# Layer 0's keys and values by seven sub-products, in the order that layer 1 has

## The chip, the core and the metric

The kernel runs on one core of one Trainium2 chip. Five engines work side by side and wait for one another by semaphores: TensorE (PE, matmuls; PEld is its weight load), VectorE (DVE), ScalarE (ACT), GpSimd (POOL, here mostly an issuer of DMAs) and SyncE (SP, the other issuer of DMAs). The metric is the device time of one launch in microseconds; lower is better.

## The reference

Two layers of a decoder on 512 tokens of width 1024, all in float32. The part that the change touches is the attention branch of a layer and what lies around it:

```python
mod = (c_act @ w_ada + b_ada)[:, None, :]
sh1, sc1, g1, sh2, sc2, g2 = jnp.split(mod, 6, axis=-1)
h = rmsnorm(x, norm1_w) * (1 + sc1) + sh1
u = h @ w_in
u_pool, u_conv, b_conv, c_conv, q, k, v, gate_logits = jnp.split(u, offsets, axis=-1)
y_pool = pool_mixer(u_pool, pool_w, pool_scale)
y_conv = b_conv * causal_short_conv(c_conv * u_conv, conv_w)
q = apply_partial_rope(rmsnorm(q.reshape(B, S, ATTN_HEADS, HEAD_DIM), q_norm_w), cos, sin)
k = apply_partial_rope(rmsnorm(k.reshape(B, S, ATTN_HEADS, HEAD_DIM), k_norm_w), cos, sin)
o = moba_attention(q.transpose(0, 2, 1, 3), k.transpose(0, 2, 1, 3), v.transpose(0, 2, 1, 3))
gates = jax.nn.sigmoid(gate_logits).reshape(B, S, N_BRANCH, D)
merged = (gates[:, :, 0] * (y_pool @ p_pool) + gates[:, :, 1] * (y_conv @ p_conv)
          + gates[:, :, 2] * (y_attn @ p_attn))
x = x + g1 * (merged @ w_out)
h2 = rmsnorm(x, norm2_w) * (1 + sc2) + sh2
x = x + g2 * ((jax.nn.silu(h2 @ w_gate) * (h2 @ w_up)) @ w_down)
```

Keys and values together are h (512 x 1024) times 1024 columns of w_in.

## The kernel before

**Matmuls.** Every float32 operand is split into a high part, rounded to the matmul's own format, and a low part, the rest. A product is three matmuls (`mm3`): high x high, high x low, low x high. Weights come in tiles of eight 128 x 128 blocks (512 KB). For most tiles SP fetches the tile into a `raw` buffer (three of them, `RAW`), ACT writes the high part `whi` (L407) and DVE the low part `wlo` (L410); of each there are five buffers. For columns 20 and up of w_in (21 and up in layer 1) the low part is made otherwise (`split_by_transfer`): ACT writes minus the high part (L429) and a DMA from POOL's queue adds the tile to it (L431). `next_w` hands out the tiles in a fixed order and keeps three or four loaded ahead.

**Order.** The program is written out by hand and traced in order; a scheduler then sets each engine's own order by priority, which is the order of the text, among what it holds ready. DVE's weight splits, its dots (below) and a few others are pinned: among themselves they stay in the order of the text. Each engine runs its list strictly in that order.

**Ticks.** A tick falls every 2048 columns of `mm3`, so every four `mm3` of 512 columns, or 12 matmuls. At a tick the attention's parts (`fibers`) are moved on and the queue `bulk` of small jobs is served: its credit grows by `bulk_rate`, to at most 4, and jobs are let out while the credit is not negative; each costs what it is listed with. A column tile of w_in against h (`feature_tile`, so also a gate) is eight `mm3`, two ticks.

**Dots.** The modulation vectors are made on DVE: for each of the six parts (SH1, SC1, G1, SH2, SC2, G2) eight dots, each a 512 KB tile of w_ada (fetched by SP) times c, summed along the row (L513), and a small end job (L546, L550). A dot is a job of cost 1.2, an end one of 0.2. Dots with `early` put their tile into a `raw` buffer, the others into one of six `w4` buffers.

**A layer's stages.** First q and three more columns; then three column tiles for the convolution and pool; then keys and values; then attention, whose small matmuls are laid among gate tiles, the products of the pool and convolution branches, and more gates; then the last gates and the attention branch in the order of `GATE2` (six gates, attention blocks 0 and 1, gates 6 and 7, attention blocks 2 to 7). Each attention block is one tick on PE, and on DVE a gating (L1270), a sum (L1307) and the low part of the sum (L679); its result is `merged[j]`. Then the output projection (`tail`), whose first tile reads all eight of `merged`, and whose result is scaled by G1 (L1313).

**Layer 1** is in `JOINT`: its keys and values are made by `keys_values`. Both operands are cut into two by two blocks and seven products of blocks are made for eight (Winograd's form of Strassen), called B21, B11, R1, -V, B22, T3 and T4 in this order. DVE makes the sums of blocks of h (`sums_one`, `sums_two`), which read the whole h (`norm.h`, written by ACT beside the high part when `Norm` has forms); the sums of blocks of weights are made by DMAs that add (`summed`) and by DVE (L345). The convolution, the rest of the pool and the pool's weights come only after the keys and values, four gates are made ahead (`ready`), attention is started after five ticks for three, and the dots of G1 are queued at the first attention block of `GATE2` with rate 1.1 and the credit at 0.

**Layer 0** makes keys, then values, by `wide()`: 96 matmuls of 512 columns each. The dots of G1 stand in `bulk` during them, the rotary tables (`rotary`, small DVE instructions and two sines on ACT) in `bulk` before them. After the products of the convolution branch, the dots of SC2 and SH2 are queued at rate 0.27.

**Roots.** `rsqrt_small` gives the 1/sqrt of the squares of q and k (128 x 64), in both layers, by a bit trick and four steps of Newton on DVE: 15 instructions.

Of the kernel before, what the change touches and what calls it, by code (L numbers as in the profile page):

```python
# [12 lines left out]
F32 = mybir.dt.float32  # L13
# [47 lines left out]

JOINT = (1,)

# [22 lines left out]
def hybrid_trunk(ctx, tc, xT, ws, ada, cols, pool_w, qk_w, crow, pos, con, out):  # L86
# [22 lines left out]
    def ps_mm():  # L109
        return psum.tile([P, S], F32, tag="mm", name=nm("mm"), bufs=4)  # L110
# [323 lines left out]
    def by_transfer(l, blocks):  # L434
        return len(blocks) == KT and blocks[0][0] == "in" and blocks[0][2] >= (21 if l in JOINT else 20)

# [148 lines left out]
    class Norm:  # L585
# [81 lines left out]
        def first_lo(self, k):  # L667
            pin(V.scalar_tensor_tensor(self.lo[k], self.t, mod[0][:, SH1, k:k + 1], f32(self.hi[k]),
                                       op0=ALU.add, op1=ALU.subtract))

        def k(self, k):
# [28 lines left out]
    def rsqrt_small(ss, shape, n):  # L700

        v, y, t = sm(shape, tag="rq", bufs=3), sm(shape, tag="rq", bufs=3), sm(shape, tag="rq", bufs=3)
        V.tensor_scalar(v, ss, 1.0 / n, EPS, op0=ALU.mult, op1=ALU.add)
        yi = y.bitcast(I32)
        V.tensor_scalar(yi, v.bitcast(I32), 1, None, op0=ALU.arith_shift_right)
        V.tensor_scalar(yi, yi, -1.0, float(0x5F3759DF), op0=ALU.mult, op1=ALU.add)
        for _ in range(4):
            V.tensor_mul(t, v, y)
            V.scalar_tensor_tensor(t, t, -0.5, y, op0=ALU.mult, op1=ALU.mult)
            V.scalar_tensor_tensor(y, t, 1.5, y, op0=ALU.add, op1=ALU.mult)  # L710
        return y
# [163 lines left out]
    scratch = ps_pair()  # L875
    norm = Norm(forms=False)

# [76 lines left out]
    for l in range(L):  # L954
# [187 lines left out]
        def conv_chain(j, z):  # L1142
# [7 lines left out]
            bulk.append((1.3, go))  # L1150

        joint = l in JOINT
        bulk_rate[0] = 1.4
# [9 lines left out]
        for j in range(2):  # L1163
# [15 lines left out]
            if not joint:  # L1179
                conv_chain(j, z)  # L1180
                if j == 1:
                    bulk.append((0, lambda: pool_chain(1, pool1)))

        y_pool, y_conv = [], []
# [47 lines left out]

        def gate():
            g = ps_mm()
            feature_tile(g, next_w())
            sg = bigt(F32)
            A.activation(sg, g, AF.Tanh, scale=0.5)
            return sg

        m01, y_attn = [], []  # L1240
# [20 lines left out]
        if l == 0:  # L1261
            bulk.extend(ada_tasks(l, (SC2, SH2), True))
        bulk_rate[0] = 0.27
        ahead_now[0] = 3
# [361 lines left out]
```

## Time and profile before

| | us |
|---|---|
| median of 3 runs | 1433.7 |
| lowest and highest | 1433.33, 1436.47 |
| profiled execution: span from first to last instruction | 1431.7 |
| PE busy in it | 1426.4 |
| DVE busy in it | 1038.3 |
| ACT busy in it | 731.3 |
| POOL busy in it | 153.2 |

The profiled execution's own time is known by its span, 2.0 us under the median of the runs shown; what lies outside the span is not on the page. Views of the trace used below: the page; the chain of waits (the work that ended last, followed back); groups of instructions by line, with count, busy time and mean duration in ns; the timeline of one engine in a stretch, with start and duration in us; windows, which give each engine's busy time in a stretch; and the waits. Matmuls overlap in PE's pipeline, so the pace of PE is read from starts, or from a row of the chain, not from the mean duration of one matmul.

### The profile page before, as it was taken

The numbers are of one execution on the slowest core, as the hardware profiler recorded it, in microseconds if no ns is written. First come the engines' busy times: TensorE is split into PE (matmuls) and PEld (weight loads), VectorE is DVE, ScalarE is ACT, GpSimd is POOL, SyncE is SP. The second block draws the span as 40 slices with busy tenths as digits, with TensorE's granted clock in tenths as the row PEclk, the third lists the DMA queues.
The fourth block names the chain that finished last, engine by engine and source line by source line (L and its number), as shares of the span: only waits on it lengthen the run. The fifth ranks groups of instructions, "written<-read, shape, count | busy, mean of one in ns | idle before, by whom it ended". The sixth has DMA issues, their size and how long they took to land.

```text
span 1431.7 us, 22037 instructions
## 1 busy us (share of the span) xinstructions
PE 1426.4 (100%) x8340; PEld 1258.8 (88%) x8340; DVE 1038.3 (73%) x1904; ACT 731.3 (51%) x1229; POOL 153.2 (11%) x215
## 2 busy tenths in 40 slices
PE   9999999999999999999999999999999999999999
PEld 8888888888988998989988888888889989999997
DVE  8887777649686767677788996655878747657663
ACT  5635666733653452535454675666336525435450
POOL 0000110101100311211002000010020103111200
PEclk9999999999999999999999999999999999999999
DMA  9547876765346766756537665567672537636522
GB/s 372 207 147 210 217 189 164 191 220 164 91 141 217 192 175 206 186 144 207 187 103 234 174 152 143 133 163 179 257 206 85 141 103 193 175 105 176 139 89 83
DMA packets 92378, 245.51 MB, mean 171 GB/s; under 512 B 11752, under 2 KB 24432, under 8 KB 92272
## 3 DMA queue, kind: packets, MB, share of 16 engines
q1 hardware_dynamic: 67312, 177.37, 36.4%
q0 software_dynamic: 24368, 66.60, 23.3%
q8 instruction: 65, 1.06, 0.3%
q14 instruction: 41, 0.34, 0.1%
q10 hardware_dynamic: 592, 0.14, 0.0%
HBM read 241.97 MB, written 2.10 MB: 170 GB/s over the span
## 4 chain that ended last, share of the span: by engine, by line
PE 99%; DMA 0%; DVE 0%; SPq 0%; ACT 0%; issue 0%; DVEq 0%; ACTq 0%
PE mm L157 84%; PE pair L157 13%; PE mm L163 2%; DMA x<-in_xT 0%; SPq L203 0%; DVE w L513 0%; ACT big L665 0%; DVE big L917 0%; DVE big L907 0%; DVE tmp L661 0%; DVE x L1313 0%; ACT rst L932 0%; DVE rst L935 0%; DVE rst L934 0%; DVE rst L936 0%
## 5 line engine op out<-in xcount | busy, mean ns | idle before, releaser
L157 PE MATMUL mm<-big,whi 128*128 128x512 f32 (+1 forms) x4334 | 1072.9, 339 | 0.0
L157 PEld LDWEIGHTS mm<-big,whi 128*128 128x128 f32 x4334 | 741.4, 190 | 85.2 <-issue 2.6
L157 PE MATMUL mm<-big,wlo 128*128 128x512 f32 (+1 forms) x2167 | 732.0, 338 | 0.0
L157 PEld LDWEIGHTS mm<-big,wlo 128*128 128x128 f32 x2167 | 411.1, 190 | 45.0 <-issue 0.4
L407 ACT ACTIVATE whi<-raw 128x1024 fp32r<-128x1024 f32 (+2 forms) x190 | 195.9, 1034 | 199.3 <-PE mm L157 112.2
L410 DVE TENSOR_TENSOR wlo<-raw,whi 128x1024 fp32r<-128x1024 f32 (+2 forms) x190 | 223.5, 1187 | 43.8 <-ACT whi L407 43.3
L407 ACT ACTIVATE whi<-w 128x1024 fp32r<-128x1024 f32 x78 | 82.5, 1058 | 150.9 <-PE mm L157 91.5
L1313 DVE SCALAR_TENSOR_TENSOR x<-mm,mod,x 128x512 f32<-128x512 f32 (+1 forms) x89 | 61.5, 693 | 76.4 <-PE mm L157 76.3
L410 DVE TENSOR_TENSOR wlo<-w,whi 128x1024 fp32r<-128x1024 f32 x78 | 94.0, 1221 | 30.4 <-ACT whi L407 29.7
L513 DVE SCALAR_TENSOR_TENSOR w<-w,csil 128x1024 f32<-128x1024 f32 x80 | 95.7, 1220 | 13.9 <-DMA w<-in_ada 13.7
L268 POOL DMA_DIRECT2D w<-in_ws x72 | 46.6, 660 | 475.7 <-DVE wlo L410 278.5
L431 POOL DMA_DIRECT2D wlo<-in_ws x47 | 40.1, 854 | 401.9 <-ACT wlo L429 262.3
L270 POOL DMA_DIRECT2D w<-in_ws x72 | 63.2, 890 | 150.6 <-DMA w<-in_ws 148.3
L157 PE MATMUL pair<-whi,big 128*128 128x512 f32 x240 | 79.2, 389 | 0.0
L157 PE MATMUL pair<-big,whi 128*128 128x256 f32 (+1 forms) x392 | 78.9, 298 | 0.0
L157 PEld LDWEIGHTS pair<-big,whi 128*128 128x128 f32 x392 | 63.4, 191 | 2.8
L427 ACT ACTIVATE whi<-raw 128x1024 fp32r<-128x1024 f32 x47 | 50.1, 1066 | 30.6 <-PE mm L157 18.1
L157 PE MATMUL pair<-big,wlo 128*128 128x256 f32 (+1 forms) x196 | 58.4, 298 | 0.0
L157 PEld LDWEIGHTS pair<-whi,big 128*128 128x128 f32 x240 | 45.1, 188 | 9.3
L1270 DVE SCALAR_TENSOR_TENSOR big<-big,mm 128x512 f32<-128x512 f32 x48 | 32.6, 684 | 25.4 <-PE mm L157 24.8
L429 ACT ACTIVATE wlo<-whi 128x1024 fp32r<-128x1024 f32 x47 | 49.6, 1057 | 0.5
L679 DVE TENSOR_TENSOR big<-tmp,big 128x512 fp32r<-128x512 f32 x48 | 33.0, 691 | 21.3 <-ACT big L678 20.4
(244 smaller groups left out, 1402.6 us busy)
## 6 DMA issues: line engine op xcount, KB each, us to landing
raw<-in_ws SPq DMA_DIRECT2D x146, 512.0 KB, 4.3
w<-in_ada SPq DMA_DIRECT2D x80, 512.0 KB, 5.8
w<-in_ws POOLq DMA_DIRECT2D x144, 256.0 KB, 4.7
wlo<-in_ws POOLq DMA_DIRECT2D x47, 512.0 KB, 7.1
raw<-in_ws SPq DMA_DIRECT2D x64, 256.0 KB, 3.8
raw<-in_ws SPq DMA_DIRECT2D x24, 384.0 KB, 3.6
raw<-in_ada SPq DMA_DIRECT2D x16, 512.0 KB, 4.6
raw<-in_ws SPq DMA_DIRECT2D x16, 448.0 KB, 5.7
```

The source lines that it names most:

```text
L157: tc.keep_in_program_order(T.matmul(*a, **k))
L268: nc.gpsimd.dma_start(dst, self.source(0, 1))
L270: nc.gpsimd.dma_start(dst, self.source(*other), accum_op=ALU.add)
L407: A.activation(hi[:, :n], raw[:, :n], AF.Copy)
L410: ins = V.tensor_sub(lo[:, :n], raw[:, :n], f32(hi)[:, :n])
L427: A.activation(hi[:, :n], raw[:, :n], AF.Copy)
L429: A.activation(lo[:, :n], f32(hi)[:, :n], AF.Copy, scale=-1.0)
L431: nc.gpsimd.dma_start(lo[:, i:i + m].rearrange("p b n -> p (b n)"), src, accum_op=ALU.add)
L513: return V.scalar_tensor_tensor(aw, aw, 1.0, csil, op0=ALU.mult, op1=ALU.mult, accum_out=mod[l][:, part, j:j + 1])
L679: last_split[0] = V.tensor_sub(lo, src, f32(hi))
L1270: V.scalar_tensor_tensor(sg, sg, 1.0, branch, op0=ALU.add, op1=ALU.mult)
L1313: V.scalar_tensor_tensor(x[k][:, lo:hi], src, mod[l][:, part, k:k + 1], x[k][:, lo:hi], op0=ALU.mult, op1=ALU.add)
```

## The change

- `JOINT = (0, 1)`: layer 0 takes layer 1's way through keys and values, with all that hangs on it in the order of the text.
- `by_transfer`: still from column 20 in layer 0 and 21 in layer 1.
- The first `Norm` gets its forms: eight tiles `h` more, each written by ACT after the low part of its tile.
- `rotary()` is called after the convolution's columns and before keys and values, no longer from `bulk`.
- `rsqrt_small`, in both layers: ScalarE's Abs_reciprocal_sqrt, then two steps of Newton of three DVE instructions each.
- Where layer 0 queues the dots of SC2 and SH2, the credit is set to 0.
- `gate()` is only defined earlier in the text.

```diff
-JOINT = (1,)
+JOINT = (0, 1)
...
-        return len(blocks) == KT and blocks[0][0] == "in" and blocks[0][2] >= (21 if l in JOINT else 20)
+        return len(blocks) == KT and blocks[0][0] == "in" and blocks[0][2] >= (21 if l > 0 else 20)
...
         def first_lo(self, k):
             pin(V.scalar_tensor_tensor(self.lo[k], self.t, mod[0][:, SH1, k:k + 1], f32(self.hi[k]),
                                        op0=ALU.add, op1=ALU.subtract))
+            A.activation(self.h[k], self.t, AF.Identity, bias=mod[0][:, SH1, k:k + 1])
...
-        v, y, t = sm(shape, tag="rq", bufs=3), sm(shape, tag="rq", bufs=3), sm(shape, tag="rq", bufs=3)
-        V.tensor_scalar(v, ss, 1.0 / n, EPS, op0=ALU.mult, op1=ALU.add)
-        yi = y.bitcast(I32)
-        V.tensor_scalar(yi, v.bitcast(I32), 1, None, op0=ALU.arith_shift_right)
-        V.tensor_scalar(yi, yi, -1.0, float(0x5F3759DF), op0=ALU.mult, op1=ALU.add)
-        for _ in range(4):
-            V.tensor_mul(t, v, y)
-            V.scalar_tensor_tensor(t, t, -0.5, y, op0=ALU.mult, op1=ALU.mult)
+        y, t = sm(shape, tag="rq", bufs=3), sm(shape, tag="rq", bufs=3)
+        A.activation(y, ss, AF.Abs_reciprocal_sqrt, bias=epst, scale=1.0 / n)
+        for _ in range(2):
+            V.scalar_tensor_tensor(t, ss, n * EPS, y, op0=ALU.add, op1=ALU.mult)
+            V.scalar_tensor_tensor(t, t, -0.5 / n, y, op0=ALU.mult, op1=ALU.mult)
             V.scalar_tensor_tensor(y, t, 1.5, y, op0=ALU.add, op1=ALU.mult)
...
-    norm = Norm(forms=False)
+    norm = Norm()
...
                 if j == 1:
                     bulk.append((0, lambda: pool_chain(1, pool1)))
+        if l == 0:
+            rotary()
...
         if l == 0:
             bulk.extend(ada_tasks(l, (SC2, SH2), True))
+            credit[0] = 0.0
         bulk_rate[0] = 0.27
```

What `joint` switches on for layer 0, in lines that the diff leaves as they are:

```python
if joint:
    bulk.append((0.4, pool_weights))
    for j in range(2):
        conv_chain(j, zs[j])
    pool_chain(1, pool1)
    bulk_rate[0] = 1.6
    ready = [gate() for _ in range(3)]
    flush_bulk()
...
        if j == 0:
            drain()
            if joint:
                bulk.extend(ada_tasks(l, (G1,)))
                bulk_rate[0], credit[0] = 1.1, 0.0
```

More of the change, by code (lines that the diff above doesn't have):

```diff
@@ L1150, in conv_chain, with gate @@
             bulk.append((1.3, go))
+        def gate():
+            g = ps_mm()
+            feature_tile(g, next_w())
+            sg = bigt(F32)
+            A.activation(sg, g, AF.Tanh, scale=0.5)
+            return sg
         joint = l in JOINT
@@ L1231, in hybrid_trunk @@
         flush_bulk()
[L1233 to L1238, printed above, removed]
         m01, y_attn = [], []
```

## The prediction

> **What bounds the kernel now.** I read the page first, then the list of what PE waited for, then the chain of waits around both layers' keys and values.
>
> ```profile
> span 1431.7 us, 22037 instructions
> PE 1426.4 (100%) x8340; PEld 1258.8 (88%) x8340; DVE 1038.3 (73%) x1904; ACT 731.3 (51%) x1229; POOL 153.2 (11%) x215
> PEclk9999999999999999999999999999999999999999
> PE 99%; DMA 0%; DVE 0%; SPq 0%; ACT 0%; issue 0%; DVEq 0%; ACTq 0%
> ...
> PE pair L157 <- POOL ones L214: 1.1, 1, 1.1
> PE pair L157 <- ACT ccol L882: 0.3, 1, 0.3
> PE mm L157 <- ACT big L665: 0.2, 1, 0.2
> ```
>
> The first line to see is the chain: 99% of what ended last is PE. The last three lines are all that PE waited for, 1.6 us, before the layers are under way. The clock is full throughout. So the time is the sum of PE's matmuls: a matmul taken out is worth its full pace, and any other edit costs only what it makes PE wait. The execution's span is 1431.7, the runs' median 1433.7; I work with differences and subtract them from the median.
>
> **The matmuls removed.** Layer 0's two `wide()` are 2 x 4 tiles x 8 k x 3 = 192 matmuls of 512 columns; seven products of 24 are 168.
>
> ```profile
> core 0: us, PE busy (x) PEld busy (x) DVE busy (x) ACT busy (x) POOL busy (x), PEclk, DMA share, GB/s
> 780.02:818.11 38.09, 38.09 (x170) 31.55 (x169) 35.65 (x63) 26.39 (x38) 6.49 (x9) 1.00 0.66 180
> 70.29:113.83 43.54, 43.54 (x194) 36.06 (x193) 35.79 (x90) 17.63 (x25) 1.84 (x2) 1.00 0.52 166
> ...
> 780.02 10.88 PE pair L157 x48
> 801.78 5.44 PE mm L157 x24
> ```
>
> The windows are layer 1's seven products and layer 0's eight (each counts two neighbours at its edge). 10.88 us for 48 is 0.2267 us a matmul, in both layers. 24 x 0.2267 = 5.44 us, which is also one product's row, and the two windows differ by 5.45. **Term 1: -5.44.**
>
> [...]
>
> **The end of layer 0's gates: more dots.** This is where I expect part of it to be lost. In layer 0 so far only the last of the 16 dots of SC2 and SH2 comes after attention block 0 (305.40 below). Counting ticks in the text of the change: from where they are queued to block 0 there are 2 (a gate) + 24 (12 gates) + 8 (branch products) + 12 (six gates) = 46 ticks of 0.27 = 12.4 of credit, from 0 where it was 4. That lets out 11 dots and one end job. Five dots of SH2 are left, and eight of G1 come on top: 13 dots, at rate 1.1 about one a tick, for 12 ticks. Layer 1 has eight there, all out by block 3; layer 0 would have one before each of blocks 2, 3, 4, 5 and 7, and two after.
>
> ```profile
> 1009.81 1.22 DVE L513 SCALAR_TENSOR_TENSOR w<-w,csil 128x1024 f32<-128x1024 f32 x1
> 1010.95 0.08 DVE L513 DVE_READ_ACCUMULATOR w<-w,csil 128x1 f32 x1
> ...
> 1013.67 1.22 DVE L410 TENSOR_TENSOR wlo<-raw,whi 128x1024 fp32r<-128x1024 f32 x1
> ...
> 1021.66 1.22 DVE L513 SCALAR_TENSOR_TENSOR w<-w,csil 128x1024 f32<-128x1024 f32 x1
> 1022.80 0.08 DVE L513 DVE_READ_ACCUMULATOR w<-w,csil 128x1 f32 x1
> 1023.41 0.69 DVE L1270 SCALAR_TENSOR_TENSOR big<-big,mm 128x512 f32<-128x512 f32 x1 [0.53 <-PE mm L157]
> ...
> 1025.52 0.69 DVE L679 TENSOR_TENSOR big<-big,big 128x512 fp32r<-128x512 f32 x1 [0.70 <-ACT big L678]
> 1026.13 1.22 DVE L513 SCALAR_TENSOR_TENSOR w<-w,csil 128x1024 f32<-128x1024 f32 x1
> ...
> 1038.45 1.37 DVE L679 TENSOR_TENSOR big<-big,big 128x512 fp32r<-128x512 f32 x2
> ...
> 1041.57 0.62 PE L157 MATMUL mm<-big,whi 128*128 128x512 f32 x2
> ...
> 305.40 1.22 DVE L513 SCALAR_TENSOR_TENSOR raw<-raw,csil 128x1024 f32<-128x1024 f32 x1
> ...
> raw<-in_ws SPq DMA_DIRECT2D x146, 512.0 KB, 4.3
> raw<-in_ada SPq DMA_DIRECT2D x16, 512.0 KB, 4.6
> DMA to landing us min/median/max: 3.1/4.2/6.7
> ```
>
> These are DVE's timeline in layer 1 from block 1 on, PE's row at which the first output tile comes to `merged[7]`, the one dot that layer 0 has there now (305.40), and SP's fetches with the median time to landing (the last row is of the eleven weight fetches in layer 1 from 985 to 1045). A dot holds DVE 1.14 us (1009.81 to 1010.95). From block 2 (1023.41) DVE has only the 0.7 idle before 1025.52. The last low part is done at 1039.8, PE reads it at 1041.57 + 0.23 = 1041.8: layer 1 has 2.0 us to spare.
>
> - *Lower end.* The new layer 0 has three more dots between block 2 and the last low part (blocks 3, 4, 5, 7 against 3). The last low part comes 3 x 1.14 = 3.4 later, or 2.7 if the idle 0.7 takes it up; PE waits 0.7 to 1.4.
> - *Upper end.* The five dots of SH2 use `raw` buffers. With three, each tile takes the buffer of the one three before it. The order is SH24, weights 4-5, SH25, SH26, weights 6-7, SH27, weights of the output. Weights 6-7 get the buffer of weights 4-5, free when the split at 1013.67 ends, 1014.8; 4.3 to land and 1.06 for ACT make 1020.2. Before it DVE has two dots, to 1017.1, and then stands, since splits and dots are pinned. Five pieces of 1.14 follow, to 1025.9, where layer 1 is through at 1022.9: 2.5 later for block 2. With the 2.7 above the last low part is at 1045.0 and PE waits 3.2.
>
> I take 2.0, nearer the upper end, since the medians of the landings put the buffers in force; the shortest landing, 3.1, would take 1.2 off. **Term 2: +2.0** (0.7 to 3.2). Behind the late dots wait G1's end job and the first scaling (L1313); the output tiles have four PSUM banks, 3 x 5.44 us of room, so that costs nothing.
>
> **Keys and values: DVE full, and a late transfer.**
>
> ```profile
> 780.00:830.00 50.00, 50.00 (x222) 41.12 (x221) 47.56 (x93) 32.86 (x50) 6.82 (x10) 1.00 0.71 186
> ...
> 800.03 2.35 DVE L410 TENSOR_TENSOR wlo<-w,whi 128x1024 fp32r<-128x1024 f32 x2
> ...
> 67.44 0.16 DVE L566 CAST posf<-post 128x4 f32<-128x4 int32 x1
> 67.64 0.19 DVE L568 TENSOR_TENSOR ang<-posf,cont 128x32 f32<-128x32 f32 x1
> ...
> L431 POOL DMA_DIRECT2D wlo<-in_ws x2: 837/848/858, 816.0 to 816.9; - x2
> DMA to landing us min/median/max: 7.9/8.6/9.4
> L429 ACT ACTIVATE wlo<-whi 128x1024 fp32r<-128x1024 f32 x47 | 49.6, 1057 | 0.5
> ```
>
> DVE is busy 47.56 of 50 us there, and PE waits for none of it. The closest is B22: of its two splits (800.03) the first ends at 801.2, and PE needs it at 801.78 + 0.23: 0.8 to spare. Layer 0 adds the rotary tables, 18 instructions at 0.2 = 3.6 us, and two weight splits, 2.3, that layer 1 has behind it by then; it has no dots of a next layer beside them, and its convolution moves out of the way. None of it standing in idle time, PE would wait 5.9 - 0.8 = 5.1; all of it, 0. Layer 1's own DVE idles 2.4 us in the seven products (35.65 of 38.09, above), and layer 0's has no other work to do there, so I take 0. Gate column 20 is read at 818.11 and its low part now comes by POOL's DMA, 8.6 us after issue; its buffers are free at 807.2 (the end of B22), and ACT's two passes of 1.06 make the issue 809.4 and the landing 818.0: just in time. Should ACT take it after the root, which waits for the squares until 810.9, it lands some 4 us late. I take 0, as PE first needs it 0.45 after 818.11. **Term 3: 0** (0 to 5.1).
>
> **Roots, h, G1.**
>
> ```profile
> 810.88 0.20 DVE L703 TENSOR_SCALAR rq<-ssq 128x64 f32<-128x64 f32 x1
> ...
> 815.18 0.17 DVE L1194 TENSOR_SCALAR nrq<-rq 128x32 f32<-128x32 f32 x1
> ...
> L709 DVE SCALAR_TENSOR_TENSOR rq<-rq,rq 128x64 f32<-128x64 f32 x8 | 1.8, 226 | 0.3
> L185 ACT ACT_TABLE_LOAD x7 | 9.0, 1283 | 1.5 <-PEq L1618 1.4
> L655 ACT ACTIVATE big<-tmp,mod 128x512 f32<-128x512 f32 x15 | 10.6, 709 | 0.0
> 28.00:36.00 8.00, 8.00 (x37) 6.64 (x36) 8.00 (x13) 4.11 (x7) 0.00 (x0) 1.00 1.03 409
> ```
>
> The root now takes 4.3 us (810.88 to 815.18); after, one activation (under L655's 0.71) and six steps at 0.26 (0.226 and the gap) are about 2.3, and in layer 0 a table switch of 1.28 more, as the sines stand before it. It is shorter in both, and PE does not wait for it now, so 0; the first gates cover it. [...]
>
> In the first stage DVE is the full engine (8.00 of 8), ACT has 3.9 of 8 free, and the eight writes of h (0.71 each, one in 4.6 us) stand behind work that PE needs: 0, at most 0.7 once. The eight dots of G1 leave the stretch of `wide()`, where nothing waited for them.
>
> **Sum.** 1433.7 - 5.44 + 2.0 + 0 = **1430.3**.
>
> **Rivals.**
> - *All hidden.* The scheduler finds idle time for the dots and term 2 is 0.5 or less: 1433.7 - 5.44 + 0.2 = 1428.5. For it: PE waits for nothing now, also in layer 1, which does all but five of the dots. Against: the 2.0 to spare is less than three dots.
> - *Keys and values late.* Term 3 is 2.5 to 5 beside some of term 2: 1433.7 - 5.44 + 5 = 1433.3. For: 0.8 to spare in a full DVE. Against: shorter roots, and layer 1 as pattern.
> - *Slower.* The `raw` buffers in the gates' end: two landings follow each other there (SH26 and weights 6-7, then SH27 and the output's weights), and each microsecond by which they are longer is one of DVE's and so of PE's. At 9 us a landing, as POOL's transfers take, against 4.5, term 2 is 3.2 + 2 x 4.5 = 12.2: 1440.5. It decides the sign for this measurement from a term 2 of 8.3, landings over 7.1. Against: SP's rows say 4.3 and 4.6, 6.7 at the longest.
> - That the change does not do what it says has no room here: 24 matmuls fewer are in the text.
>
> **Numbers.** What this measurement can tell from no change is 0.2%, 2.9 us, so faster is under 1430.8. Forecast (1429.3 to 1431.5) 0.42, two thirds of it faster; all hidden 0.27; keys and values late 0.23; slower 0.08. Faster 0.55, the same 0.37, slower 0.08. The range 1428.0 to 1434.0 takes in the first three but for their tails.
>
> **What would show it.** PE with 8316 matmuls; layer 0's stretch of keys and values 38.1 us; in the list of PE's waits a new line behind L678 or L679 near 330 us, of 0.7 to 3.2; 13 L513 between block 0 of layer 0 and its output tiles; no wait of PE between 65 and 115 us. Wrong would be a PE that waits for a `wlo` in the first 120 us, or none at 330.

## The result: slower, by two stalls that the sum had at 0 and at 2 us

| | before | after |
|---|---|---|
| median of 4 runs each, same chip, us | 1433.51 | 1445.63 |
| lowest to highest | 1432.83 to 1436.47 | 1444.32 to 1446.9 |
| span of the profiled execution | 1431.7 | 1444.5 |

The ratio is 1.0082 (95% interval 1.0069 to 1.0094): slower, where 1430.3 was forecast. In the changed kernel's trace some lines have moved by one: L679 and L680 are the high part (ACT) and the low part (DVE) of a sum, L1271 is the gating, L1308 the sum of the branches. First the page of the changed kernel (span, busy time, and by engine the chain that ended last):

```profile
span 1444.5 us, 22085 instructions
PE 1427.9 (99%) x8316; PEld 1257.2 (87%) x8316; DVE 1060.5 (73%) x1930; ACT 749.6 (52%) x1260; POOL 163.5 (11%) x227
PE 90%; DVE 5%; DMA 3%; ACT 1%; issue 0%; SPq 0%; ACTq 0%; DVEq 0%
```

and its list of what PE waited for (total, times, longest):

```profile
PE mm L157 <- DVE wlo L410: 6.0, 1, 6.0
PE mm L157 <- ACT big L679: 2.8, 2, 1.7
PE mm L157 <- DVE big L1271: 1.8, 1, 1.8
...
PE mm L157 <- DVE big L680: 0.5, 2, 0.2
```

The matmuls are 24 fewer (8340 - 8316). But the chain, 99% PE before, now runs 9% through DVE, DMA and ACT, and there are two new places: one wait for a weight's low part, and a group behind the gating and the sums. PE's timeline in the changed kernel (start, duration, instructions, and in brackets the idle time before and its releaser) shows the first:

```profile
80.93 0.39 PE L157 MATMUL mm<-whi,big 128*128 128x512 f32 x1
87.36 0.80 PE L157 MATMUL mm<-wlo,big 128*128 128x512 f32 x1 [6.04 <-DVE wlo L410]
87.95 1.05 PE L157 MATMUL mm<-whi,big 128*128 128x512 f32 x2
...
91.75 0.62 PE L157 MATMUL mm<-whi,big 128*128 128x512 f32 x2
```

and two windows of it (columns as in the prediction) show both:

```profile
87.00:91.50 4.50, 4.14 (x10) 3.28 (x11) 4.50 (x6) 1.69 (x2) 0.00 (x0) 0.50 0.32 98
332.00:352.00 20.00, 14.94 (x48) 10.66 (x47) 19.14 (x32) 7.13 (x10) 0.00 (x0) 0.83 0.64 208
```

**First stall, 81 us.** Between two starts lie 6.43 us for 0.23: 6.2 lost. The ten matmuls after it (87.36 to 91.75) take 4.39 us for 10 x 0.2267 = 2.27: another 2.1 lost, and the window's granted clock is 0.50. Together **8.3 us**, at the product R1. **Second stall, 332 to 352 us.** 48 matmuls begin in 20 us in which an undisturbed kernel has 90 (below): 42 x 0.2267 = **9.5 us**, with a clock of 0.83. The waits for L679, L1271 and L680 come to 5.1 in the list (2.8 + 1.8 + 0.5) and to 6.1 by the starts; some 3.3 more are 18 matmuls behind the waits that take 7.3 us for 4.1 (11 from 337.06 to 341.25, 7 from 347.98 to 351.13). The books close: -5.4 + 8.3 + 9.5 = +12.4 of the 12.8 by which the spans differ.

What DVE did ahead of the first stall, from its timeline in the changed kernel:

```profile
79.16 0.69 DVE L1182 TENSOR_TENSOR big<-mm,big 128x512 f32<-128x512 f32 x1
79.76 0.16 DVE L566 CAST posf<-post 128x4 f32<-128x4 int32 x1
...
81.99 0.18 DVE L582 COPY sins<-sins 128x32 f32<-128x32 f32 x1 [0.30 <-ACT sins L581]
...
86.00 0.18 DVE L582 COPY cosc<-cosc 128x32 f32<-128x32 f32 x1
86.08 1.22 DVE L410 TENSOR_TENSOR wlo<-w,whi 128x1024 fp32r<-128x1024 f32 x1
```

PE needs that L410 at 81.16. DVE finishes the convolution's product (L1182) at 79.8 and then, by its fixed order, does all of the rotary work, with four low parts of T3 and T4 let in between: 6.3 us. Earlier it had stood idle, as a window of the same kernel shows:

```profile
54.00:64.00 10.00, 10.00 (x46) 8.29 (x45) 5.39 (x8) 4.79 (x7) 0.00 (x0) 1.00 0.96 278
```

DVE is busy 5.4 of 10 us. At the head of its list stand splits of B21's weights, which come late; this is the fetch that SP issues at 51.48, in the view of the DMAs (the last number is the time to landing):

```profile
raw<-in_ws SPq DMA_DIRECT2D x1, 512.0 KB, 10.6
```

It takes 10.6 us, where the prediction had a median of 4.3; the second summands of POOL's sums of weights for R1 (L322, issued at 49.2 and 51.6) land in the same microseconds, after 8.8 and 10.3 us.

For the second stall, the dots between 303 and 351 us in the changed kernel (grouped by line; count, shortest, median and longest in ns, first and last start):

```profile
L513 DVE SCALAR_TENSOR_TENSOR w<-w,csil x8: 1215/1218/1221, 325.3 to 349.0; 128x1024 f32<-128x1024 f32 x8
L513 DVE SCALAR_TENSOR_TENSOR raw<-raw,csil x5: 1217/1221/1227, 303.9 to 324.0; 128x1024 f32<-128x1024 f32 x5
```

The 13 dots are there as counted, five of them in `raw` buffers. ACT's timeline, with its two instructions after 303 us:

```profile
311.78 1.06 ACT L407 ACTIVATE whi<-raw 128x1024 fp32r<-128x1024 f32 x1 [8.57 <-DMA raw<-in_ws]
312.75 0.62 ACT L679 ACTIVATE big<-big 128x512 fp32r<-128x512 f32 x1
```

and the fetches that SP issues between 302 and 305.5, with their median to landing:

```profile
raw<-in_ada SPq DMA_DIRECT2D x2, 512.0 KB, 7.7
raw<-in_ws SPq DMA_DIRECT2D x1, 512.0 KB, 7.7
```

They land after 7.7 us. ACT stands 8.6 us for the weights, and the high part of `merged[0]` (L679) stands behind it, with DVE's low parts behind that. From 314 on DVE is late and stays so. The chain of waits between 300 and 352 us has three of SP's fetches on it (start, time to landing):

```profile
304.04 7.72 DMA raw<-in_ws
...
318.44 3.19 DMA raw<-in_ws
...
325.23 4.64 DMA raw<-in_ws
```

In the order that the prediction gives, these are weights 4-5, weights 6-7 and weights of the output. Only the first lands late; it is issued when the split of an earlier tile, which ends at 304.0, has freed its `raw` buffer.

### The profile page after: what moved, and what is told of

It reads as the page before. It is cut to its first block, busy times and chain, and to the rows that moved or that the text cites. A ratio compares the mean times of both kernels' runs of the same rounds, so it can differ in the third digit from the quotient of the medians.

```text
span 1444.5 us, 22085 instructions
## 1 busy us (share of the span) xinstructions
PE 1427.9 (99%) x8316; PEld 1257.2 (87%) x8316; DVE 1060.5 (73%) x1930; ACT 749.6 (52%) x1260; POOL 163.5 (11%) x227
## 4 chain that ended last, share of the span: by engine, by line
PE 90%; DVE 5%; DMA 3%; ACT 1%; issue 0%; SPq 0%; ACTq 0%; DVEq 0%
PE mm L157 78%; PE pair L157 11%; DMA raw<-in_ws 2%; PE mm L163 2%; DVE wlo L410 1%; DVE w L513 1%; ACT whi L407 1%; DVE big L680 1%; ACT big L679 0%; DMA x<-in_xT 0%; DVE tmp L661 0%; DVE big L668 0%; DVE big L1308 0%; DVE raw L513 0%; SPq L203 0%
## 5 line engine op out<-in xcount | busy, mean ns | idle before, releaser
L410 DVE TENSOR_TENSOR wlo<-raw,whi 128x1024 fp32r<-128x1024 f32 (+2 forms) x188 | 221.4, 1187 | 48.6 <-ACT whi L407 48.1
L407 ACT ACTIVATE whi<-w 128x1024 fp32r<-128x1024 f32 x84 | 88.9, 1058 | 153.7 <-PE mm L157 87.2
L410 DVE TENSOR_TENSOR wlo<-w,whi 128x1024 fp32r<-128x1024 f32 x84 | 101.3, 1221 | 29.8 <-ACT whi L407 29.2
L513 DVE SCALAR_TENSOR_TENSOR w<-w,csil 128x1024 f32<-128x1024 f32 x80 | 95.8, 1220 | 13.5 <-DMA w<-in_ada 13.4
L157 PE MATMUL pair<-whi,big 128*128 128x512 f32 x256 | 82.3, 390 | 0.0
L157 PEld LDWEIGHTS pair<-whi,big 128*128 128x128 f32 x256 | 48.1, 188 | 9.8
L679 ACT ACTIVATE big<-big 128x512 fp32r<-128x512 f32 x52 | 32.1, 626 | 42.3 <-DVE big L1308 18.2
L157 PE MATMUL pair<-wlo,big 128*128 128x512 f32 x128 | 49.2, 390 | 0.0
```

What stands on the lines that cost most here:

```text
L157: tc.keep_in_program_order(T.matmul(*a, **k))
L407: A.activation(hi[:, :n], raw[:, :n], AF.Copy)
L410: ins = V.tensor_sub(lo[:, :n], raw[:, :n], f32(hi)[:, :n])
L513: return V.scalar_tensor_tensor(aw, aw, 1.0, csil, op0=ALU.mult, op1=ALU.mult, accum_out=mod[l][:, part, j:j + 1])
L679: A.activation(hi, src, AF.Copy)
```

## The experiments

All are timed in five rounds beside the kernel before. The table gives each kernel's median, its ratio with the interval, and the time that PE lost in its profiled execution, in us by stretch: the starts of its matmuls less their full pace (0.2267 us for one of 512 columns), so waits and half clock together. In 132 to 300 the 3.0 us that the kernel before has there (among the attention's small matmuls) are taken off. A loss moves the later stretches by as much. The profiled execution is one of those timed and not always a middle one (in e12 the fastest, 1434.32, in e9 the slowest, 1452.41), so a row's losses need not add up to its median.

| run | median | ratio (95%) | 30-80 | 80-96 | 96-132 | 132-300 | 300-360 |
|---|---|---|---|---|---|---|---|
| changed kernel | 1445.63 | 1.0082 (1.0069 to 1.0094) | 0 | 8.3 | 0 | 0.3 | 9.5 |
| e2 dots spread | 1446.40 | 1.0091 (1.0075 to 1.0108) | 0 | 8.9 | 0 | 10.8 | 0 |
| e4 credit kept | 1453.52 | 1.0143 (1.0128 to 1.0158) | 0 | 8.2 | 0.6 | 10.8 | 6.9 |
| e6 G1 in the gates | 1439.29 | 1.0043 (1.0030 to 1.0057) | 0 | 7.8 | 0 | 3.0 | 0 |
| e12 G1 alone | 1436.64 | 1.0021 (1.0012 to 1.0030) | 0 | 5.5 | 0.1 | 0.4 | 0 |
| e1 rotary first | 1447.08 | 1.0099 (1.0084 to 1.0114) | 3.8 | 0.5 | 3.0 | 0.4 | 9.7 |
| e3 = e1 + e2 | 1448.16 | 1.0103 (1.0088 to 1.0118) | 5.4 | 0 | 5.3 | 10.1 | 0.1 |
| e5 rotary at the tables | 1449.86 | 1.0112 (1.0098 to 1.0126) | 0 | 2.4 | 11.0 | 0.4 | 9.0 |
| e7 = e5 + e6 | 1442.70 | 1.0059 (1.0047 to 1.0072) | 0 | 2.7 | 9.7 | 2.1 | 0 |
| e8 sums wait | 1446.90 | 1.0086 (1.0072 to 1.0099) | 0 | 7.9 | 0 | 0.5 | 11.8 |
| e9 = e1 + e8 | 1447.69 | 1.0103 (1.0089 to 1.0118) | 0 | 7.2 | 2.5 | 1.6 | 11.0 |
| e10 = e9 + G1 later | 1444.43 | 1.0071 (1.0058 to 1.0084) | 0 | 6.2 | 1.4 | 3.7 | 3.1 |
| e11 before, roots and h | 1433.79 | 1.0003 (0.9994 to 1.0012) | 0 | 0 | 1.1 | 0.7 | 0 |
| e14 = e12 + rotary in two | 1435.15 | 1.0011 (1.0002 to 1.0020) | 1.2 | 2.3 | 2.3 | 0.3 | 0 |
| e15 = e12, no rotary | 1435.11 | 1.0014 (1.0005 to 1.0023) | 0 | 1.6 | 1.8 | 0.3 | 0 |
| e16 = e12, one summand | 1432.59 | 0.9992 (0.9984 to 1.0001) | 0 | 4.1 | 0.5 | 0.3 | 0 |
| e17 = e14, late summand | 1431.27 | 0.9984 (0.9976 to 0.9993) | 0 | 0 | 3.1 | 0.3 | 0 |
| e18 rotary on POOL, late | 1433.08 | 0.9997 (0.9988 to 1.0006) | 0 | 0 | 3.6 | 0.3 | 0 |
| e19 rotary on POOL | 1433.73 | 1.0000 (0.9991 to 1.0009) | 0 | 2.9 | 3.9 | 0.4 | 0 |

### The gates' end

**e2: the dots of G1 ahead of the gates.**

```diff
-            bulk.extend(ada_tasks(l, (SC2, SH2), True))
+            bulk.extend(ada_tasks(l, (G1, SC2, SH2), True))
             credit[0] = 0.0
-        bulk_rate[0] = 0.27
+        bulk_rate[0] = 0.65
...
-                if joint:
+                if l > 0:
                     bulk.extend(ada_tasks(l, (G1,)))
```

> The changed kernel with one edit: layer 0's eight dots of G1 are queued with those of SC2 and SH2 ahead of the gates (through the raw buffers, rate 0.65 for 0.27), so that none is left for the last gates. Theory A (the waits of PE at 334 to 352 us and the half clock behind them, some 9.5 us, come of the 13 dots and their fetches that stand there): PE waits 0.5 us or less between 330 and 352 us, 1436.1 (1434 to 1438). Theory B (DVE or the weight fetches are late there whatever the dots do): 4 us or more stay, over 1441. A new cost is possible in the attention's part (240 to 300 us), where DVE gets 12 dots more: the theory says 0 to 1 us. Both expect the 6.2 us at 80 us unchanged.

The stall at the end went to 0, as theory A had it, and the time did not fall: 10.8 us came up in the attention. The expectation's "0 to 1 us" there was wrong. The list of PE's waits in e2 names them:

```profile
PE mm L157 <- DVE wlo L410: 5.7, 1, 5.7
PE mm L163 <- DVE tmp L847: 3.7, 3, 1.9
PE mm L157 <- DVE big L683: 1.2, 1, 1.2
```

L847 and L683 are steps of the attention on DVE. DVE's mean there leaves room (9.2 us busy of the 14 from 244 to 258), but not the chain from a small matmul over DVE to the next.

**e4: the credit not set to 0** (the line `credit[0] = 0.0` taken out).

> The changed kernel with one edit: the credit is not set to 0 where layer 0 queues the dots of SC2 and SH2, so it is 4 there as in the kernel before. By the count of ticks three dots more are let out ahead of the last gates, and 10 in place of 13 stand behind attention block 0. Theory A (each dot there is 1.14 us of DVE on PE's path): the waits at 334 to 352 us are 3.4 us shorter, 1442.2 (1440 to 1443.5). Theory B (the late landings of the weights there decide, not the number of dots): within 1 us of the changed kernel, 1444.6 to 1446.6. Theory C (setting the credit to 0 hides dots from the attention's start): a new wait of PE between 225 and 260 us.

Three dots fewer at the end are worth 2.6 us (9.5 to 6.9), near A's 3.4; but C came true, at 163 and 217 us (earlier than it said), with 10.8 us. DVE's timeline in e4 there:

```profile
214.27 0.69 DVE L1270 SCALAR_TENSOR_TENSOR big<-big,mm 128x512 f32<-128x512 f32 x1 [1.71 <-PE mm L157]
219.78 1.22 DVE L513 SCALAR_TENSOR_TENSOR raw<-raw,csil 128x1024 f32<-128x1024 f32 x1 [4.82 <-DMA raw<-in_ada]
220.93 0.08 DVE L513 DVE_READ_ACCUMULATOR raw<-raw,csil 128x1 f32 x1
220.93 0.74 DVE L683 SCALAR_TENSOR_TENSOR big<-mm,colt,big 128x512 fp32r<-128x512 f32 x1
```

A dot at the head of DVE's list waits 4.8 us for its tile, with nothing else to do meanwhile, and L683, for which PE waits 4.1 us, stands behind it. So a dot can cost more than its 1.14 us: here it cost the time by which its tile was late.

**e6: G1 at the first of the last gates, the rest of SH2 after them.**

```diff
+        if l == 0:
+            bulk.extendleft(reversed(ada_tasks(l, (G1,))))
+            bulk_rate[0], credit[0] = 1.2, 0.0
         for step, j in GATE2:
```

At attention block 0 of layer 0 the rate is set to 0, so nothing more is let out there, and at the output tiles the rate is 1.2 for 0.9.

> The changed kernel with one edit: layer 0's eight dots of G1 are queued, ahead of what is left of SH2, at the first of the six last gates (about 300 us), rate 1.2, and not at attention block 0; the rest of SH2 waits for the output tiles, with the dots of G2, rate 1.2 there. In the changed kernel DVE is busy 12.7 of the 20 us from 300 to 320 and 17.5 of those from 320 to 340. Theory A (the loss at 334 to 352 is DVE work that stands where DVE is full, and its place is those idle 7 us): it falls from 9.5 us to 2 or less, and the output tiles lose nothing: 1437.5 (1436 to 1440). Theory B (the landings of the weights in raw buffers, 8 to 12 us there, decide): the fetches only come together earlier, 4 us or more of waits remain between 300 and 360 us, over 1441.

A: 9.5 to 0, 6.3 us off the median, with 2.7 us more in the attention's last part, where G1's dots now begin (270 us, earlier than meant).

**e12: only G1's eight dots behind block 0; what is left of SH2 goes to the output tiles.**

```diff
                 if joint:
+                    rest = list(bulk)
+                    bulk.clear()
                     bulk.extend(ada_tasks(l, (G1,)))
...
         flush_bulk()
+        bulk.extend(rest)
...
-        bulk_rate[0] = 0.9
+        bulk_rate[0] = 0.9 if l > 0 else 1.2
```

> The changed kernel with one edit: what is left of layer 0's dots of SH2 at attention block 0 waits for the output tiles, and only G1's eight dots stand behind block 0, as in layer 1. Theory A (the five dots of SH2, which take the weights' raw buffers, are what layer 0 has more than layer 1, where nothing waits): the 9.5 us at 334 to 352 fall to 2 or less, 1437.5 (1436 to 1439). Theory B (eight dots are too many as well, since the transfers of G1's tiles still land beside the weights): 4 us or more stay, over 1440.

A, and the cleanest run of this part: the whole second stall goes, and nothing comes in its place. PE's list of waits has one line beyond those of the kernel before:

```profile
PE mm L157 <- DVE wlo L410: 3.6, 1, 3.6
```

The window of the gates' end is undisturbed:

```profile
332.00:352.00 20.00, 20.00 (x90) 16.55 (x89) 17.54 (x28) 7.13 (x10) 0.00 (x0) 1.00 0.70 228
```

And the weights' fetches issued from 299.9 to 301.5 are (the view of the DMAs)

```profile
raw<-in_ws SPq DMA_DIRECT2D x2, 512.0 KB, 7.9
```

So the weights take as long to land as in the changed kernel (7.9 against 7.7), and PE waits for nothing: neither such landings nor G1's eight dots make the stall by themselves; it takes the five dots of SH2 as well. How they do it is read from the traces. In e12 they hold no `raw` buffer ahead of the weights, and ACT's timeline is

```profile
304.02 0.63 ACT L679 ACTIVATE big<-big 128x512 fp32r<-128x512 f32 x1 [2.70 <-DVE big L1310]
307.82 1.06 ACT L407 ACTIVATE whi<-raw 128x1024 fp32r<-128x1024 f32 x1 [3.17 <-DMA raw<-in_ws]
308.79 0.61 ACT L679 ACTIVATE big<-big 128x512 fp32r<-128x512 f32 x1
```

The high part of `merged[0]` (304.02) stands ahead of the late weights here and not behind them, as it does in layer 1 of the kernel before. In e6 it stands behind them as in the changed kernel, and with two dots in place of thirteen from there on PE loses nothing. So ACT's order alone does not make the stall either. What the five dots' time on DVE, their buffers and ACT's order are each worth, no run shows.

### The wait at 81 us

**e1: rotary ahead of the convolution's columns** (the call moved up).

> The changed kernel (median 1445.6, span 1444.5) with one edit: the rotary tables of layer 0 are called before its convolution and pool columns and not after them. Theory A (the wait of 6.2 us ahead of R1 is DVE's order: the pinned rotary instructions, with their wait for ScalarE's sine, stand ahead of the split of R1's first weights): the wait for a wlo of L410 between 75 and 95 us falls to 0.5 us or less and the stretch at half clock behind it goes, 8.3 us together, so 1437.3 (1436 to 1439). Theory B (DVE is late there because it stood 4 us behind weights that landed late, and the order only shows it): 4 us or more of the wait stay, 1441 to 1446. Both expect the waits at 334 to 352 us unchanged.

The wait at 81 went, as A said; 3.8 us came at 65 and 3.0 behind 96, and the time did not fall (1447.08). DVE's timeline in e1 has

```profile
64.33 0.18 DVE L582 COPY sins<-sins 128x32 f32<-128x32 f32 x1 [5.53 <-ACT sins L581]
```

and ACT's

```profile
61.69 1.06 ACT L407 ACTIVATE whi<-raw 128x1024 fp32r<-128x1024 f32 x1 [2.80 <-DMA raw<-in_ws]
62.77 1.28 ACT L581 ACT_TABLE_LOAD   x1
64.07 0.23 ACT L581 ACTIVATE sins<-rope 128x32 f32<-128x32 f32 x1
```

DVE waits 5.5 us for a sine, which waits on ACT behind a high part that waits for the late weights, and behind a table switch. The splits are pinned behind the copy.

**e3: e1 and e2 together.**

> The changed kernel with both edits: rotary tables ahead of the convolution's columns, and layer 0's dots of G1 queued ahead of the gates at rate 0.65. If the two stalls are apart and are all that the change lost: 1445.6 - 8.3 - 9.5 = 1427.8 (1427 to 1431), which is the time before less the 24 matmuls, 1433.5 - 5.4 = 1428.1; PE's chain is 99% PE again and PE waits for 2 us in all. If a third loss stands behind them: over 1431.

Over 1431: both stalls are gone from their places, but the losses that e1 and e2 brought elsewhere add up (5.4 and 5.3 us in the first stretches, 10.1 in the attention).

**e5: rotary just ahead of the tables.**

> The changed kernel with one edit: layer 0's rotary tables are made just before they are read, behind the product -V, and not ahead of B21. The earlier move (ahead of the convolution's columns) took away the wait at 81 us and brought 3.6 us at 65 and 3.0 behind 96: DVE was given the same work in a stretch that was as full. Theory A (DVE has its idle time behind 96 us, 4 us of 22, so the rotary work is free there and nowhere before): the 8.3 us at 80 to 92 us go but for at most 1, and no wait over 0.5 us comes in their place: 1437.8 (1436.5 to 1439). Theory B (DVE is short of time in the whole stretch, wherever the rotary work stands): 4 us or more of waits remain between 60 and 135 us, over 1441.

B by its numbers (13.4 us from 80 to 132, 1449.86): the stretch 80 to 96 came down to 2.4 us, but a wait of 4.7 came at 105, again a split of weights behind the second sine's copy, here with the root between the two copies (DVE waits 1.1 us for it at 105), and a wait of 2.6 us for a transfer comes on top. The 4 us of idle time were no place here for work that waits for another engine.

**e7: e5 and e6.**

> The changed kernel with both: rotary tables behind -V, and G1's dots at the last gates. If both theories A hold: 1445.6 - 7.8 - 8.1 = 1429.7 (1428 to 1432), faster than the kernel before (1433.1), which is the change's 24 matmuls without what was lost. If one of them fails: 1437 to 1439. If both: over 1441.

Over 1441, but not since both failed: the end of the gates held (0 at 300 to 360), with 2.1 us lost in the attention, and rotary's new place lost more than expected, 12.4 us from 80 to 132, much as in e5.

**e8: the sums for R1 wait for B21's first split.**

```diff
-            if sub == 2:
+            if sub == (2 if self.l else 1):
                 self.x = [w4([P, C_BLOCKS, P]) for _ in range(2)]
                 for i in range(2):
+                    if not self.l:
+                        pin(V.memset(self.x[i][:, 0, :1], 0.0))
                     self.summed(self.x[i], (1, 1), i)
```

> The changed kernel with one edit: in layer 0 the two sums of weight blocks for R1 are fetched only when DVE has split B21's first weights (a write of one column per tile, 0.06 us on DVE, makes POOL's transfers wait for it), so that they do not land together with B21's and B11's weights. In the changed kernel those landings took 8.8 to 10.6 us and DVE stood idle for 4.3 us at 57 to 63. Theory A (part of the wait at 81 us is that idle time): DVE idles less than 1.5 us there, the 6.2 us fall to 3 or less, 1441 to 1442.5. Theory B (only the order of rotary and split counts): 5 us or more stay, 1444.5 to 1446.5. If the sums now come too late: a wait for a DMA or for L410 of over 6 us at 81, over 1446.5.

R1 waits as long as B has it (5.5 us in the list), but the time is over B's range, and the trace speaks for the last case, sums that come too late. A window of e8 (its lines are two higher):

```profile
54.00:64.00 10.00, 10.00 (x46) 8.29 (x45) 8.94 (x17) 5.92 (x9) 1.24 (x2) 1.00 0.56 184
```

DVE was busy 8.9 of these 10 us, so the idle time was filled. But then the sums came late, two transfers one after another, of which the first took 8.2 us to land; ACT's timeline:

```profile
72.60 1.06 ACT L409 ACTIVATE whi<-w 128x1024 fp32r<-128x1024 f32 x1 [3.42 <-DMA w<-in_ws]
73.56 0.61 ACT L681 ACTIVATE big<-big 128x512 fp32r<-128x512 f32 x1
```

ACT stood 3.4 us for them, with the high part of a sum of h (L681) behind. The late landing had only changed its tile.

**e9 and e10: e1 with e8, and G1's dots at the third gate.**

> The changed kernel with two edits together: the rotary tables ahead of the convolution's columns, and the sums of weight blocks for R1 fetched only after the split of B21's first weights. Alone the first moved the wait from 81 us to 65 (3.6 us) and 96 to 135 (5.4 us), the second did nothing for the time although DVE's idle 4.3 us at 57 to 63 were filled. Theory A (rotary's 18 instructions need idle time of DVE that is there only when no split waits for late weights: ScalarE's sine stood behind a high part that waited for its transfer till 61.7): the wait at 65 us goes, what is left between 60 and 135 us is 2 us or less, and the time 1438.5 (1437 to 1440). Theory B (DVE is short of time in this stretch, 3.6 us of rotary and 2.3 of splits that layer 1 does not have there): 5 us or more of waits remain, at whichever place, 1442 to 1447.

> As the run before, and G1's eight dots of layer 0 queued at the third of the six last gates (two gates later than in the run that took the 9.5 us at the end away and left 2.5 us of waits in the attention's last part), rate 1.2, up to attention block 2, the rest of SH2 at the output tiles. If the 9.5 us go and the two gates of delay spare the 2.5 us: 9 us less than the run before, 1429.5 (1428 to 1432) under theory A of that run, 1433 to 1438 under its theory B.

B by the waits in both: 9.7 and 7.6 us stay in the first stretches, with times above B's ranges (1447.69, 1444.43). In e9 the sums are again what is late: ACT waits 4.8 us for them, till 80.8. e10's dots lose 3.1 us at the gates.

**e11: the kernel before with the roots and h alone.**

> The kernel before with two parts of the change alone: the roots by ScalarE with two steps of Newton, and the eight tiles h of the first norm (written and, in layer 0, read by nobody). The prediction took both at 0 (h at most 0.7): 1433.5 (1432.5 to 1434.5), PE waits as in the kernel before. If the table switches or ScalarE's extra 5.7 us in the first stage cost: over 1435.

No change that can be told from none (0.9994 to 1.0012): these parts cost about 0 here, as predicted. The 1.1 us at 96 to 132 are of its profiled execution, the slowest of its eleven.

At this point e12 held a hint: its text is the changed kernel's up to 300 us, yet it lost 5.5 us at 81 and not 8.3, in an execution in which B21's weights landed sooner. Its view of the DMAs has for that fetch

```profile
raw<-in_ws SPq DMA_DIRECT2D x1, 512.0 KB, 8.2
```

where the changed kernel has 10.6. Five kernels share the text up to there, and in their profiled executions PE's wait follows this landing:

| | changed kernel | e2 | e4 | e6 | e12 |
|---|---|---|---|---|---|
| B21's weights to landing, us | 10.6 | 10.3 | 10.2 | 9.8 | 8.2 |
| PE's wait for L410 at 81 us | 6.0 | 5.7 | 5.6 | 5.2 | 3.6 |

So in this range each microsecond of landing is one of PE's wait. The last six runs, all on e12, part rotary from landing.

**e14: rotary in two parts**, the arithmetic early and the sines late:

```diff
+        if l == 0:
+            rotary()
         for j in range(2):
...
         def tables():
+            if l == 0:
+                sines()
```

> The kernel with G1's dots alone behind block 0, and one more edit: rotary in two parts. Its 16 instructions on DVE that wait for nothing stand ahead of the convolution's columns (where DVE idles some 4 us for late weights), the two sines on ScalarE and the two copies behind them only at the tables, behind -V. Theory A (what cost PE, wherever rotary stood, was DVE's fixed order standing behind a sine, ScalarE's table switch and a split that waits): no wait over 1.5 us between 60 and 135 us, some 3 us of waits in all as in the run with rotary at the tables (2.4 at 80 to 96), 1431.5 (1430 to 1433), faster than the kernel before. Theory B (DVE's amount of work is too much for the stretch): 5 us or more in all remain, over 1434.

**e15: no rotary.**

> The kernel with G1's dots alone behind block 0, and rotary left out: the tables are filled by two writes at the start (so q and k are not turned). It measures what layer 0's keys and values lose without the rotary work. Theory A (rotary is the cause of the wait at 81 us): the waits between 60 and 135 us come to 3 us or less, 1431 (1429.5 to 1432.5), as in the run with rotary in two parts. Theory C (late weights are the cause and rotary only rides on them): 5 us or more remain, over 1434.

**e16: the sums without their second summand.**

> The kernel with G1's dots alone behind block 0, and layer 0's two weight sums for R1 fetched without their second summand (two transfers of 512 KB less between 49 and 62 us; the keys and values are then not the reference's). Two executions of the same text gave a wait of 6.2 us with B21's second weights landing at 62.0 and of 3.8 with 59.7. Theory A (the wait at 81 us carries the landing one to one): they land in 5 us, by 57, and the wait is 1 to 2 us, 1432 to 1434. Theory B (rotary alone): 4 us or more of wait, 1435.5 to 1437.5.

Each took off a part: 5.5 us at 80 to 96 came down to 2.3 (e14), 1.6 (e15) and 4.1 (e16). By its numbers e14 is B; the other two come out between their theories: e15 has C's time with waits near A's (3.4 us for 3); e16 has A's time with a longer wait (2.4 us) than A had. At R1 itself e14 and e15 do not wait at all, though the weights land in 10.3 and 9.8 us; their losses stand later, at 93 to 96. e16 still waits there 2.4 us with the weights landed in 4.2. So without rotary ahead of R1's split the wait at 81 goes, and with it there early weights only shorten it. e15's time is no measure of rotary's amount: with the tables ready at the start, PE waits 2.8 us for the first norm's high parts (L668 in its list; 0.2 for L665 in the kernel before), ahead of the table's columns. In the medians e16 gains the most: 0.9992 (0.9984 to 1.0001) beside 1.0011 (1.0002 to 1.0020) for e14, timed on the same chip.

**e17: both, with nothing left out.** e14 with its first part one column later, and of the sums, called as early as in e8, only the second summand made to wait:

```diff
             nc.gpsimd.dma_start(flat, self.source(0, 1, cp))
+            if behind:
+                pin(V.tensor_copy(flat[:, :1], flat[:, :1]))
```

> The kernel with G1's dots alone behind block 0 and rotary in two parts, the first of them now one column later (ahead of the second pair of the convolution's columns), and the second summands of R1's two sums fetched only when DVE has split B21's first weights (a copy of one column in place, on DVE). The run with rotary in two parts left 5.8 us of waits between 30 and 132 us, with B21's second weights landing in 10.4 us; the run without second summands had them in 4.3. Theory A (both, late weights and rotary's order, make the loss): landing under 6 us, 3 us or less of waits, 1432.5 (1431 to 1433.5). Theory B (the stretch has too little DVE time whatever lands when): 5 us or more, 1434.5 to 1437.

A (3.1 us lost, 1431.27), and faster than both kernels: 0.9984 (0.9976 to 0.9993) of the kernel before. B21's weights in its view of the DMAs:

```profile
raw<-in_ws SPq DMA_DIRECT2D x1, 512.0 KB, 4.6
```

Two of its windows:

```profile
54.00:64.00 10.00, 10.00 (x46) 8.29 (x45) 8.73 (x20) 6.36 (x9) 1.79 (x2) 1.00 0.53 151
80.00:96.00 16.00, 16.00 (x72) 13.25 (x71) 15.47 (x20) 12.73 (x20) 0.00 (x0) 1.00 0.42 131
```

They land in 4.6 us, DVE is busy 8.7 of the 10 us, and at 80 to 96 PE does not wait: 72 matmuls begin in 16 us. The largest line left in PE's list of waits is

```profile
PE mm L157 <- DMA wlo<-in_ws: 1.6, 1, 1.6
```

This is the low part that POOL's transfer makes for a gate column behind the keys and values.

**e18 and e19: rotary's arithmetic on POOL**, with and without the late summand.

> The kernel with G1's dots alone behind block 0, rotary's arithmetic up to the sines on GpSimd at the start (its fused multiply-adds as a multiply and an add), sines and copies at the tables, and R1's second summands fetched behind the split of B21's first weights as in the run before. DVE has 3.4 us less to do and no late weights. Theory A: 2.5 us or less of waits between 30 and 132 us, 1431.5 (1430 to 1432.5), under the kernel before. Theory B: as the run with rotary left out, 3.4 us or more, 1434 to 1436.

> As the run before, but R1's sums are fetched as in the changed kernel. Rotary is off DVE and the weights land late: as the run with rotary left out, 3.4 us of waits between 30 and 132 us, 1434.8 (1433.5 to 1436). The difference to the run before is the landing's share when rotary is gone: 2 to 3 us if both count, under 1 if rotary alone counts.

Theory A of e18 missed: 3.6 us stayed where it had 2.5 or less, at 1433.08. e19's time is in its range with twice the loss expected (6.8 us for 3.4). At 80 to 96 the landing's share is 2.9 us with rotary off DVE (e19 against e18), as expected; in the medians it is 0.65 us, and the intervals overlap (0.9988 to 1.0006, 0.9991 to 1.0009). Neither beats e17, though DVE has 3.4 us less to do, so what is left there is not DVE's amount of work. Why the last 3 to 4 us at 96 to 132 stay was not tried.

## Why the prediction was wrong, step by step

- **Term 1 (-5.44)** held: 24 matmuls fewer, and in e17 the stretch without a stall.
- **Term 3 (0, range 0 to 5.1)** is the step that failed: 8.3. It asked whether DVE's amount of work fits, and took layer 1 as the pattern. Three things were missing. Layer 1 has no rotary work, and here it stands in a pinned list between the sums and R1's first split (6.3 us), with ACT's sines inside. The landing of B21's weights was in no term, though POOL's sums for R1 are fetched beside them (10.6 us; DVE idles 4.6 of 10), and each microsecond of it was one of PE's wait (five executions, above). And the half clock behind a wait, 2.1 us, was in no term. e17, which mends order and landing and keeps the work, brings the place to 0; e16, e15 and e14, which mend one, leave 1.6 to 4.1. The late transfer for the gate column, taken at 0, is the 1.6 us that shows in e17 once the stall ahead of it is gone.
- **Term 2 (+2.0, range 0.7 to 3.2)** had the place and the dots right and the size wrong: 9.5, of which 6.1 are waits. The count (13 dots, five through `raw`) and the place (behind L679, L680 and the gating, at 335) were as written. The chain through `raw` runs as the upper end has it, but it starts late. The step that failed is its first: the split of weights 4-5 was taken from layer 1 (1013.67, some 6.6 us behind block 0's gating), and in the changed kernel it comes at 317.15, 11.8 us behind (305.34). That tile's fetch waits for a buffer, lands after 7.7 us, and ACT stands 8.6 us for it with the high part of `merged[0]` behind. From there on the upper end is about right: weights 6-7 land in 3.2 us (4.3 was taken), and DVE stands 2.1 us before their split (3.1 was taken). The 3.3 us of slower pace behind the waits were in no term. e12 shows the price: without the five dots, 0.
- ***Slower*** had landings as the cause, with 3.2 + 2 x (landing - 4.5), and was given 0.08 on the strength of a median over the whole program. At 7.7 us its formula gives 9.6, where 9.5 was measured; that is luck. It counts the landings of SH26 with weights 6-7 and of SH27 with the output's weights, and the weights of these took 3.2 and 4.6 us. The late one was a tile earlier, and a third of the 9.5 is slower pace, which the formula does not hold.
- **Roots, h at 0**: right (e11).
- **What would show it.** "A PE that waits for a `wlo` in the first 120 us" was named as what would be wrong, and is what came.
- **The rivals.** *Keys and values late* had the first stall's side, at 2.5 to 5; *Slower* the second's, and neither reaches the time alone. They were taken as alternatives, each with the other term at its middle, where both came at once.

## What to carry to other kernels

When a stage is copied from one place to another, compare what lands beside it and what else is queued on its engines there, not only the sum of its work: take landings from the stretch (10.6 and 7.7 us here), not from the program's median (4.3). Work in a fixed order that holds a step of another engine (here a sine) is better cut there: the part that waits for nothing goes into idle time, the rest to its reader. Here the ratio was 1.0021 uncut (e12) and 1.0011 cut (e14), with intervals that overlap, and 0.9984 with the late summand as well (e17). And a dot, a split or any filler at the head of a strict list can cost as much as its transfer is late (4.8 us in e4); so put fillers where the readers behind them are not on the path (e12: 9.5 us to 0), before adding rate or credit (e2, e4: 10.8 us in the attention).

## What the runs showed of the hardware

**Half clock behind a wait.** In the changed kernel ten matmuls after the wait of 6.2 us ran at some 0.43 us for 0.2267. Windows of it at a granted clock of 0.50:

```profile
84.90:91.60 6.70, 4.24 (x10) 3.38 (x11) 6.70 (x10) 2.65 (x5) 0.00 (x0) 0.50 0.23 72
337.50:340.80 3.30, 3.30 (x10) 2.52 (x9) 3.30 (x6) 2.18 (x3) 0.00 (x0) 0.50 0.68 220
347.80:351.10 3.30, 3.12 (x7) 2.48 (x8) 3.23 (x8) 1.97 (x3) 0.00 (x0) 0.50 0.54 191
```

The windows beside them (81.2 to 84.8, 91.8 to 95, 334.9 to 337.4, 340.9 to 347.6, 351.2 to 354) have 1.00. So the first stretch is 6.7 to 7.0 us long and began while PE still waited; the other two are 3.3 to 3.6 us long, behind a wait of 2.0 us at 335 and waits of 1.3 and 1.8 us at 343 and 345. But in e1 a wait of 3.6 us at 65 was followed by none; the clock of this window of e1 is 1.00:

```profile
64.00:80.00 16.00, 12.53 (x55) 10.02 (x54) 14.35 (x33) 7.24 (x12) 5.11 (x8) 1.00 0.60 187
```

Nor was one of 2.0 us in e18 (for the gate column's `wlo`), where the window from 96 to 132 us has 1.00 as well. So the length of a wait does not tell by itself whether half clock follows: a wait of 2.0 us had it behind it once and once not, and one of 3.6 us did not. What decides it no run shows. So a wait of 2 us here costs 2 or, with a stretch of half clock behind it, about 4 (an estimate: 2.0 and nine matmuls at 0.43 for 0.2267).

**Landings vary between executions, and PE's wait with them.** The same fetch of B21's weights took 8.2 to 10.6 us in five executions whose text is the same up to there, and PE's wait followed it (3.6 to 6.0 us, table above). e12's eleven runs lie between 1434.3 and 1438.1; the landing of 8.2 us is that of the fastest of them, and of the others none is known.
